# A two-layer decoder trunk on one core: convolution taps behind the second group of attention scores instead of ahead of the first, and the last memory queries transposed within the attention

## The chip, the cores and the metric

The kernel runs on one NeuronCore of a Trainium2 chip. The core has a matrix engine (TensorE, PE in the profile, with PEld for its weight loads), a vector engine (VectorE, DVE), a scalar engine (ScalarE, ACT), GpSimd (POOL) and a queue engine (SyncE, SP) that only issues transfers. Each engine works through its own list of instructions in order and waits at an instruction until what it needs is there. The metric is the device time of one execution in microseconds; lower is better.

## The reference

Two layers. Each has a half-step feed-forward block, a mixer, a second half-step feed-forward block and a closing norm. The mixer projects 512 tokens once and splits the columns among three groups of heads:

```python
def reference(x, mem, ...):
    for l in range(DEPTH):                                     # 2 layers, 512 tokens x 1024
        h = x + 0.5 * swiglu(rms_norm(x, ffn1_norm[l]), ...)   # 1024 -> 2816 -> 1024
        p = rms_norm(h, mix_norm[l]) @ w_in[l]
        u_conv, q, k, v, q_mem = jnp.split(p, splits, axis=-1)
        y_conv = conv_module(u_conv, ...)          # GLU, 31 causal taps on 384 channels, LayerNorm, silu
        y_swa = sliding_window_attention(q, k, v, sinks)       # 6 heads of 64, window 128
        y_mem = memory_attention(qm, mk, mv)                   # 4 heads of 64 on 256 memory tokens
        h = h + jnp.concatenate([y_conv, y_swa, y_mem], -1) @ w_out[l]
        h = h + 0.5 * swiglu(rms_norm(h, ffn2_norm[l]), ...)
        x = rms_norm(h, final_norm[l])
```

## The kernel before

All products with weights are made as three float32r matmuls of split operands (`mm3`, lines 177 to 179: high by high, high by low, low by high). The feed-forward blocks take most of the time and are PE's; the change is in the mixer (`mixer`), once in each layer.

The mixer's work is written in the order of a table, `ORDER`. `c` is half of a convolution channel group's projection (`conv_half`), `q` the projection of the attention's queries and keys of a block of 128 tokens (`queries`), `Q` their transposition into columns (`query_columns`), `v` the projection of the values and of the memory's queries of a block (`values`), `V` the transposition of that block's memory queries (`value_columns`, line 573 on PE), `g0` and `g1` the scores of the first two groups of heads (`begin`), `a` the attention, `t0` to `t2` the taps of a channel group, `s` what follows the convolution (`swish`).

The attention runs over ten groups (`GROUPS`). "r" groups are memory attention on two pairs of heads, "w" groups window attention on one to three pairs. For each group PE makes scores (line 755, behind masks of line 749 for "w"), DVE takes their maxima (lines 759 or 774) and turns them into a bias (lines 760, or 775 and 776), which also needs the norm factor `rm` that POOL raises to a power (line 546). Then, pair by pair, ACT takes the exponential (line 786), PE transposes it (line 792), ACT evicts the transposes into the ring `ptb` (line 794), and PE multiplies them with the values in narrow products of 65 columns (line 803). DVE divides (lines 812 to 817), PE transposes the result (line 826), and ACT and DVE split it into an operand (lines 146 and 147). Each group's scores are made while the group before is worked on.

The 31 taps on each of three channel groups are 93 instructions of DVE over 128 x 512 (line 912 the first of a channel group, line 919 the others). A tap's place is set by hand. The taps are numbered 0 to 92 through the three channel groups. Those below `EARLY` may go as soon as their input is there; the others are put behind the bias of a score group (`biased`), as many behind each group as `LATER` says, and the rest behind the last one. A scheduler fixes each engine's list when the program is built, within these ties.

The memory queries of block t are written by ACT (line 721, out of the same PSUM tile as the values, line 719) into `scratch[0]`, 256 columns for each block, and read by PE for their transposition (line 573). The ring `ptb` is made of the two halves of the same `scratch[0]`. So the transposes of blocks 2 and 3 have to be done before `ptb` gets its second half. Block 2's were at `V2`, ahead of the attention, block 3's within the attention, behind the transposes of the first pair of the first group.

When the last tap is done, POOL adds up the three channel groups (lines 925 and 926), PE sums over the channels (line 930), and DVE, ACT and PE make the norm, while PE goes on with the output projection of the attention's part (`out_rows`).

Of the kernel before, what the change touches and what calls it, by code (L numbers as in the profile page):

```python
# [43 lines left out]
MAGIC = 12582912.0  # L44


ORDER = "c00 c01 q0 c10 q1 c11 Q0 q2 q3 Q1 c20 c21 Q2 v0 Q3 v1 V0 V1 g0 g1 v2 v3 V2 a t0 t1 t2 s"

EARLY = 50
LATER = (5, 5, 4, 4, 3, 3, 3, 3, 3, 3)  # L50


def cut(v, bits):
# [11 lines left out]
def trunk(ctx: ExitStack, tc: tile.TileContext, xT, memT, pos, w1a, w3a, w2a, w1b, w3b, w2b,  # L65
# [118 lines left out]
    def blk(k, n=P):  # L184
        return slice(k * n, (k + 1) * n)
# [383 lines left out]
    def to_columns(dst, src, n, tag="pt"):  # L569

        pt = bank([P, n, P], tag)
        for c in range(n):
            tail[0] = T.transpose(pt[:, c, :], src[:, blk(c)], ident)
        if dst is not None:
            A.activation(dst, pt[:, 0 : dst.shape[1], :], AF.Copy)
        return pt
# [38 lines left out]
    def mixer(l, x, st, last):  # L615
# [9 lines left out]
        qmT = there[:, 0:1024].rearrange("p (i s) -> p i s", i=2)  # L625
        cv = there[:, 1024:2560].rearrange("p (c s) -> p c s", c=CC)
        G.memset(vn[:, :, :, HD : HD + 1], 1.0)
        scratch = [wst.tile([P, UNIT], F32, tag="aux", name=f"aux{i}", bufs=3) for i in range(3)]
        uu = tmp.tile([P, 2, S], F32, tag="u", name="uu", bufs=1)
        query = [tmp.tile([P, 2, S], F32, tag="g", name="query", bufs=2) for _ in range(2)]  # L630
# [78 lines left out]
            keyed.append(A.activation(kT[:, blk(t)], pt[:, CC, :], AF.Copy, scale=HD**-0.5))  # L709


        def values(t):
            if not t:
                ww["v"] = [weights(wvm[l, i], 768, G if i == 2 else V, spare()) for i in range(4)]
            ps = mm() if t < 2 else bank([P, S], "po")
            with queued():
                for k in range(KD):
                    mm3(ps[:, 0:CCH], at(x, ALL, k, blk(t)), at(ww["v"][k // 2], ALL, blk(k % 2, CCH)), k == 0, k == KD - 1)
            A.activation(vn[:, t, :, 0:HD], heads(ps[:, 256:CCH]), AF.Copy, scale=rc[:, t : t + 1])
            q = scratch[0][:, blk(t, 256)]  # L720
            A.activation(q, ps[:, 0:256], AF.Copy, scale=rc[:, t : t + 1])
            head_scale(ps[:, 0:256], rc[:, t : t + 1], NM, rm[:, t, :])

        def value_columns(t):
            with queued():
                to_columns(qmT[:, :, blk(t)], scratch[0][:, blk(t, 256)], 2)

        yy, y = [], []

# [113 lines left out]
        def attention():  # L843
# [23 lines left out]
            for n, (kind, *pairs) in enumerate(GROUPS):  # L867
                ready = list(done)
                done.clear()
                final = n + 1 == len(GROUPS)  # L870
                if final:

                    for r in ready:
                        attended(*r)
                    ready = []
                elif n + 1 not in begun:
                    begin(n + 1)
                if n in (3, 5):
                    with tc.issue_after(raised[GROUPS[n - 1][0], *GROUPS[n - 1][-1]].ins):
                        out_weights(len(out_w))  # L880
                for z, (b, c) in enumerate(pairs):
                    x = turned(kind, b, c, [ps[:, z, :] for ps in begun[n][0]], begun[n][1])
                    close()
                    late = (kind, b, c, *x)
                    if not n and not z:
                        value_columns(3)
                for r in ready:
                    attended(*r)
            out_rows(0, MEMORY)
# [21 lines left out]
        def taps(c):  # L911
            V.tensor_scalar(out=cv[:, c, :], in0=ypad[:, c, 0:S], scalar1=conv_w[:, c, 0:1], scalar2=conv_b[:, c : c + 1],
                            op0=ALU.mult, op1=ALU.add)
            for j in range(1, TAPS):

                n = c * TAPS + j - EARLY
                group = sum(n >= sum(LATER[:g]) for g in range(1, len(LATER)))
# [34 lines left out]

        for step in ORDER.split():
            f = {"c": conv_half, "q": queries, "Q": query_columns, "v": values, "V": value_columns, "g": begin, "a": attention,
# [148 lines left out]
```

## Time and profile before

| | us |
|---|---|
| median of three runs (1811.9, 1816.54, 1817.14) | 1816.54 |
| the profiled execution | 1813.94 |
| its span in the trace | 1812.2 |
| of it, attention of layer 1 (444 to 512) | 68 |
| of it, attention of layer 2 (1339 to 1404) | 65 |

Two microseconds of the profiled execution lie outside its span. Times in a row are from the span's start. A timeline row has the start, the time taken, the engine, the line of the kernel, the operation, what it writes and reads, and how many instructions stand in the row; in brackets how long the engine had idled before it, and which engine, tile and line ended that. "64*128 64x256" of a matmul are its stationary and moving operand. A float32 product, as of lines 755 and 803, stands in the trace as two passes, so eight rows there are four products. PE's records overlap: in a series the distance from start to start is what one costs. The granted clock is the share of full speed that PE was given.

### The profile page before, as it was taken

How to read it: one execution, taken by the hardware profiler on the slowest of the kernel's cores; microseconds unless marked ns; L12 is line 12 of the kernel's file. 1: busy time of each engine (PE TensorE's matmuls, PEld its weight loads, DVE VectorE, ACT ScalarE, POOL GpSimd, SP SyncE). 2: the span in 40 equal slices, each digit the busy share in tenths (PEclk: the TensorE clock that was granted, in tenths of full speed). 3: DMA queues.
4: the chain of work that ended last, by engine and by line, in shares of the span. 5: the costliest groups of instructions: out<-in, count | busy, mean ns of one | idle time of the engine just before them, and what ended most of it. 6: DMA issues, size and time to landing. Idle time of an engine off the chain costs nothing.

```text
span 1812.2 us, 28077 instructions
## 1 busy us (share of the span) xinstructions
PE 1769.9 (98%) x10996; PEld 1587.2 (88%) x10996; DVE 1273.0 (70%) x1886; ACT 897.1 (50%) x1363; POOL 205.8 (11%) x225
## 2 busy tenths in 40 slices
PE   8999999999999999999999999999989999999997
PEld 6989999878778989898888898988777789898986
DVE  7969666569757857575678676666698567675755
ACT  5546444463665535353655453535446645453532
POOL 3001000024121000000010010000341210000000
PEclk9999999999899999999999999999999999999998
DMA  9456655282159456565566465643631866474622
GB/s 275 106 167 169 180 136 143 59 224 69 30 131 211 112 140 173 137 163 140 154 138 154 147 172 144 171 120 95 175 69 30 207 149 161 131 181 119 173 75 81
DMA packets 96180, 254.37 MB, mean 140 GB/s; under 512 B 9904, under 2 KB 14256, under 8 KB 96048
## 3 DMA queue, kind: packets, MB, share of 16 engines
q1 hardware_dynamic: 77040, 190.45, 34.3%
q0 software_dynamic: 19008, 62.14, 19.4%
q8 instruction: 86, 1.41, 0.3%
q14 instruction: 46, 0.38, 0.1%
HBM read 250.45 MB, written 2.10 MB: 139 GB/s over the span
## 4 chain that ended last, share of the span: by engine, by line
PE 78%; DVE 9%; issue 6%; DMA 4%; ACT 3%; SPq 0%; POOLq 0%; DVEq 0%; POOL 0%; ACTq 0%
PE mm L177 11%; PE mm L178 11%; PE mm L179 11%; PE po L177 8%; PE po L179 8%; PE po L178 8%; PE pt L177 6%; PE pt L178 6%; PE pt L179 6%; DVE there L919 3%; DVE wlo L147 1%; DMA raw<-in_wconv 1%; PE po L803 1%; DMA glo<-in_wqk 1%; ACT uu L786 1%
## 5 line engine op out<-in xcount | busy, mean ns | idle before, releaser
L146 ACT ACTIVATE whi<-raw 128x1024 fp32r<-128x1024 f32 (+3 forms) x344 | 324.6, 946 | 454.6 <-PE mm L178 232.6
L147 DVE TENSOR_TENSOR wlo<-raw,whi 128x1024 fp32r<-128x1024 f32 (+3 forms) x344 | 372.7, 1085 | 132.3 <-ACT whi L146 131.5
L178 PE MATMUL mm<-glo,whi 128*128 128x512 f32 x752 | 293.7, 391 | 1.0 <-DVE glo L147 1.0
L177 PE MATMUL mm<-ghi,whi 128*128 128x512 f32 x752 | 293.4, 392 | 0.7 <-ACT ghi L146 0.7
L179 PE MATMUL mm<-ghi,wlo 128*128 128x512 f32 x734 | 285.8, 389 | 0.0
L179 PE MATMUL po<-mh,wlo 128*128 128x256 f32 x864 | 244.6, 283 | 1.4 <-DVE wlo L147 1.4
L177 PE MATMUL po<-mh,whi 128*128 128x256 f32 x864 | 244.8, 283 | 0.0
L178 PE MATMUL po<-ml,whi 128*128 128x256 f32 x864 | 244.5, 283 | 0.0
L179 PE MATMUL pt<-xhi,wlo 128*128 128x256 f32 x864 | 244.0, 283 | 0.0
L177 PE MATMUL pt<-xhi,whi 128*128 128x256 f32 x864 | 243.3, 283 | 0.7 <-DVE g L370 0.4
L178 PE MATMUL pt<-xlo,whi 128*128 128x256 f32 x864 | 243.9, 283 | 0.0
L467 DVE SCALAR_TENSOR_TENSOR h<-mm,h 128x512 f32<-128x512 f32 x128 | 87.8, 689 | 134.6 <-PE mm L179 134.6
L178 PEld LDWEIGHTS mm<-glo,whi 128*128 128x128 f32 x752 | 141.3, 188 | 31.1 <-DVE glo L147 2.8
L177 PEld LDWEIGHTS mm<-ghi,whi 128*128 128x128 f32 x752 | 141.3, 188 | 31.1 <-ACT ghi L146 1.6
L179 PEld LDWEIGHTS po<-mh,wlo 128*128 128x128 f32 x864 | 165.8, 192 | 1.6 <-DVE wlo L147 1.6
L177 PEld LDWEIGHTS pt<-xhi,whi 128*128 128x128 f32 x864 | 165.1, 192 | 2.2 <-ACT xhi L146 0.7
L177 PEld LDWEIGHTS po<-mh,whi 128*128 128x128 f32 x864 | 165.8, 192 | 0.9 <-ACT part L389 0.2
L178 PEld LDWEIGHTS pt<-xlo,whi 128*128 128x128 f32 x864 | 165.7, 192 | 0.8
L178 PEld LDWEIGHTS po<-ml,whi 128*128 128x128 f32 x864 | 165.8, 192 | 0.6
L179 PEld LDWEIGHTS pt<-xhi,wlo 128*128 128x128 f32 x864 | 165.6, 192 | 0.0
L179 PEld LDWEIGHTS mm<-ghi,wlo 128*128 128x128 f32 x734 | 137.8, 188 | 28.7
L919 DVE SCALAR_TENSOR_TENSOR there<-ypad,par,there 128x512 f32<-128x512 f32 x180 | 135.2, 760 | 1.8
(314 smaller groups left out, 3341.8 us busy)
## 6 DMA issues: line engine op xcount, KB each, us to landing
raw<-in_w2a SPq DMA_DIRECT2D x48, 384.0 KB, 3.6
raw<-in_w2b SPq DMA_DIRECT2D x48, 384.0 KB, 3.6
raw<-in_w1b SPq DMA_DIRECT2D x26, 512.0 KB, 3.7
raw<-in_w3b SPq DMA_DIRECT2D x26, 512.0 KB, 3.9
raw<-in_w1a SPq DMA_DIRECT2D x25, 512.0 KB, 3.7
raw<-in_w3a SPq DMA_DIRECT2D x25, 512.0 KB, 4.2
wsum<-in_w1a SPq DMA_DIRECT2D x18, 512.0 KB, 4.5
wsum<-in_w3a SPq DMA_DIRECT2D x18, 512.0 KB, 4.5
```

Of the source, the lines that this page charges most:

```text
L146: A.activation(hi, x, AF.Copy)
L147: on.tensor_tensor(out=lo, in0=x, in1=hi.bitcast(F32), op=ALU.subtract)
L177: T.matmul(ps, a[0], b[0], start=first, stop=False, **more)
L178: T.matmul(ps, a[0], b[1], start=False, stop=False, **more)
L179: tail[0] = T.matmul(ps, a[1], b[0], start=False, stop=last, **more)
L467: added = V.scalar_tensor_tensor(out=h[:, d, :], in0=ps, scalar=0.5, in1=h[:, d, :], op0=ALU.mult, op1=ALU.add)
L786: raised[kind, b, c] = A.activation(pr[:, i, 0:W], scores[i], AF.Exp, bias=nm[:, b, i, c : c + 1], scale=rr[:, b, n : n + 1])
L803: tail[0] = T.matmul(po[:, 2 * c + i, :], ptb[:, i, j, :], v, start=(j == 0), stop=(j == nk - 1))
L919: V.scalar_tensor_tensor(out=cv[:, c, :], in0=ypad[:, c, j : j + S], scalar=conv_w[:, c, j : j + 1], in1=cv[:, c, :], op0=ALU.mult, op1=AL ...
```

## The change

Three things change together.

1. `EARLY` goes from 50 to 43, so seven taps fewer are free to go ahead of the first groups' maxima. `LATER` goes from (5, 5, 4, 4, 3, ...) to (1, 12, 5, 4, 3, ...): one tap behind the first group's bias in place of five, twelve behind the second's in place of five, five behind the third's in place of four; behind the last group's come 13 in place of 10.
2. `V2` leaves `ORDER`. The transposes of memory queries 2 and 3 are both made within the attention, behind the first pair of the second and of the third group.
3. The memory queries of blocks 2 and 3 are kept in a part of `query[0]`, whose earlier contents have been used by then, so that they no longer share `scratch[0]` with the ring `ptb`.

```diff
-ORDER = "... v2 v3 V2 a t0 t1 t2 s"
-EARLY = 50
-LATER = (5, 5, 4, 4, 3, 3, 3, 3, 3, 3)
+ORDER = "... v2 v3 a t0 t1 t2 s"
+EARLY = 43
+LATER = (1, 12, 5, 4, 3, 3, 3, 3, 3, 3)
...
+        def memory_query(t):
+            return (scratch[0] if t < 2 else query[0][:, 0])[:, blk(t % 2, 256)]
+
         def values(t):
...
-            q = scratch[0][:, blk(t, 256)]
+            q = memory_query(t)
...
         def value_columns(t):
             with queued():
-                to_columns(qmT[:, :, blk(t)], scratch[0][:, blk(t, 256)], 2)
+                to_columns(qmT[:, :, blk(t)], memory_query(t), 2)
...
-                    if not n and not z:
-                        value_columns(3)
+                    if n in (1, 2) and not z:
+                        value_columns(n + 1)
```

Line numbers behind line 712 are three higher in the changed kernel: 755 becomes 758, 786 789, 792 795, 803 806, 919 922.

The first place is DVE's list around the first two groups' maxima, in layer 1. `hs` and `hv` are the sums of squares of the memory queries (4240 and 4281 those of blocks 0 and 1), `there<-ypad` is a tap, `nmr` the maxima and biases of the memory groups. Before:

```order
L912 TENSOR_SCALAR there<-ypad,par 128x512
L542 TENSOR_REDUCE hs_4240<-hsq 128x4
L919 SCALAR_TENSOR_TENSOR there<-ypad,par,there 128x512
L543 TENSOR_SCALAR hv_4241<-hs_4240 128x4
L919 SCALAR_TENSOR_TENSOR there<-ypad,par,there 128x512 x3
L542 TENSOR_REDUCE hs_4281<-hsq 128x4
L919 SCALAR_TENSOR_TENSOR there<-ypad,par,there 128x512
L543 TENSOR_SCALAR hv_4282<-hs_4281 128x4
L919 SCALAR_TENSOR_TENSOR there<-ypad,par,there 128x512
L759 TENSOR_REDUCE nmr<-mm 128x2
L919 SCALAR_TENSOR_TENSOR there<-ypad,par,there 128x512
L759 TENSOR_REDUCE nmr<-mm 128x2 x2
```

With the change, from the same first row to the second group's bias and the taps behind it:

```order
L915 TENSOR_SCALAR there<-ypad,par 128x512
L542 TENSOR_REDUCE hs_4240<-hsq 128x4
L543 TENSOR_SCALAR hv_4241<-hs_4240 128x4
L542 TENSOR_REDUCE hs_4281<-hsq 128x4
L543 TENSOR_SCALAR hv_4282<-hs_4281 128x4
L762 TENSOR_REDUCE nmr<-mm 128x2 x2
L763 SCALAR_TENSOR_TENSOR nmr<-nmr,rm 128x4
L922 SCALAR_TENSOR_TENSOR there<-ypad,par,there 128x512
L762 TENSOR_REDUCE nmr<-mm 128x2
L762 TENSOR_REDUCE nmr<-cf 128x2
L763 SCALAR_TENSOR_TENSOR nmr<-nmr,rm 128x4
L922 SCALAR_TENSOR_TENSOR there<-ypad,par,there 128x512 x5
```

The six taps that stood between the first channel sum and the first maximum, and the one between the first group's two maxima, are gone from there. Twelve taps now lie between the second group's bias and the third group's maxima, mixed with the sums of blocks 2 and 3.

The second place is PE's list behind the last product of `values(3)`, and ACT's list that feeds it. `uu` and `pr` are exponentials, `mvn` the memory's values, `here` holds the queries' columns, `aux_3742` is `scratch[0]`. PE before:

```order
L179 MATMUL po<-ghi,xlo 128x384
L573 MATMUL pt<-cst,aux_3742 128x128 x2
L792 MATMUL pt<-cst,uu 128x128 x4
L573 MATMUL pt<-cst,aux_3742 128x128 x2
L792 MATMUL pt<-cst,uu 128x128 x4
L803 MATMUL po<-mvn,aux_3742 128x65 x4
L749 MATMUL mm<-maskr 128x384 x2
L755 MATMUL mm<-here 128x128 x6
```

PE with the change:

```order
L179 MATMUL po<-ghi,xlo 128x384
L795 MATMUL pt<-cst,uu 128x128 x8
L806 MATMUL po<-mvn,aux_3742 128x65 x4
L752 MATMUL mm<-maskr 128x384 x2
L758 MATMUL mm<-here 128x128 x6
L795 MATMUL pt<-cst,pr 128x128 x4
L806 MATMUL po<-mvn,aux_3742 128x65 x4
L573 MATMUL pt<-cst,query 128x128 x2
```

ACT with the change, from its table load on:

```order
L789 ACT_TABLE_LOAD
L789 ACTIVATE uu<-mm,nmr,rm 128x256 x4
L789 ACTIVATE pr<-mm,nmr,rm 128x256
L789 ACTIVATE pr<-cf,nmr,rm 128x256
L722 ACTIVATE here<-po,rc 128x2x64
L724 ACTIVATE query<-po,rc 128x256
L540 ACTIVATE hsq<-po,rc 128x256
L722 ACTIVATE here<-po,rc 128x2x64
L724 ACTIVATE query<-po,rc 128x256
L540 ACTIVATE hsq<-po,rc 128x256
L789 ACTIVATE uu<-mm,nmr,rm 128x256
L797 ACTIVATE aux_3742<-pt 128x512
```

The transposes of the memory queries have gone from between those of the exponentials, and the eight transposes of the first group follow `values(3)` at once. On ACT the rows up to the second `hsq` stand as before; the eviction of block 2's memory queries (line 575), which stood between the last `hsq` and the next exponential, has moved behind the third group's first exponentials.

The third place is DVE's list at the end of the attention, where `rd_4834` and the row L817 (L820 with the change) make the last block's result and L147 splits its transposes. Before:

```order
L813 RECIPROCAL rd_4834<-rd_4834 128x6
L919 SCALAR_TENSOR_TENSOR there<-ypad,par,there 128x512
L817 TENSOR_TENSOR aux_3743<-po,rd_4834 128x384
L147 TENSOR_TENSOR glo<-pt,ghi 128x128
L147 TENSOR_TENSOR glo<-pt,ghi 128x2x128
```

With the change:

```order
L816 RECIPROCAL rd_4834<-rd_4834 128x6
L922 SCALAR_TENSOR_TENSOR there<-ypad,par,there 128x512
L820 TENSOR_TENSOR aux_3743<-po,rd_4834 128x384
L922 SCALAR_TENSOR_TENSOR there<-ypad,par,there 128x512 x2
L147 TENSOR_TENSOR glo<-pt,ghi 128x128
L922 SCALAR_TENSOR_TENSOR there<-ypad,par,there 128x512
L147 TENSOR_TENSOR glo<-pt,ghi 128x2x128
```

The last three taps stand behind the last division instead of ahead of it.

More of the change, by code (lines that the diff above doesn't have):

```diff
@@ L44 @@
 MAGIC = 12582912.0
-ORDER = "c00 c01 q0 c10 q1 c11 Q0 q2 q3 Q1 c20 c21 Q2 v0 Q3 v1 V0 V1 g0 g1 v2 v3 V2 a t0 t1 t2 s"
-EARLY = 50
-LATER = (5, 5, 4, 4, 3, 3, 3, 3, 3, 3)
+ORDER = "c00 c01 q0 c10 q1 c11 Q0 q2 q3 Q1 c20 c21 Q2 v0 Q3 v1 V0 V1 g0 g1 v2 v3 a t0 t1 t2 s"
+EARLY = 43
+LATER = (1, 12, 5, 4, 3, 3, 3, 3, 3, 3)
 def cut(v, bits):
```

## The prediction

> **What bounds the kernel now.** I read the page first.
>
> ```profile
> span 1812.2 us, 28077 instructions
> PE 1769.9 (98%) x10996; PEld 1587.2 (88%) x10996; DVE 1273.0 (70%) x1886; ACT 897.1 (50%) x1363; POOL 205.8 (11%) x225
> ```
>
> A PE that is busy 98% of 1812.2 us leaves little to win, unless it is busy slowly somewhere. So the second view is the window table, for stretches of 3.41 us (the trace's falls and returns of the clock lie a multiple of that apart) and for the time at half clock. Columns: length, busy time of PE, weight loads, DVE, ACT, POOL, then the granted clock.
>
> ```profile
> 454.51:457.92 3.41, 1.15 (x9) 0.83 (x8) 3.13 (x7) 3.41 (x10) 0.00 (x0) 1.00 0.00 0
> 457.92:474.99 17.07, 16.30 (x76) 13.40 (x75) 9.10 (x20) 8.37 (x21) 5.33 (x5) 0.50 0.18 38
> 502.29:505.71 3.42, 2.33 (x20) 1.88 (x19) 3.42 (x8) 2.26 (x7) 0.56 (x1) 1.00 0.00 0
> 1352.21:1355.62 3.41, 1.31 (x8) 0.84 (x9) 3.18 (x7) 3.41 (x11) 1.05 (x1) 1.00 0.00 0
> 1355.62:1362.45 6.83, 6.80 (x35) 6.17 (x36) 3.30 (x9) 1.86 (x5) 1.70 (x3) 0.50 0.01 2
> 21.01:24.43 3.42, 2.50 (x15) 1.92 (x15) 3.41 (x4) 1.06 (x1) 2.45 (x3) 1.00 0.61 126
> ```
>
> In the attention of layer 1 PE runs at half clock for 17.07 us, in that of layer 2 for 6.83 us, each time behind a stretch in which it was busy 1.15 or 1.31 us of 3.41. The timeline of PE shows what emptied it; the second row below is the last product of values(3).
>
> ```profile
> 444.72 1.34 PE L755 MATMUL mm<-mT,there 64*128 64x256 f32 x9 [0.20 <-ACT there L575]
> ...
> 454.92 0.34 PE L179 MATMUL po<-ghi,xlo 128*128 128x384 f32 x1
> 457.52 0.44 PE L573 MATMUL pt<-cst,aux 128*128 128x128 f32 x2 [2.26 <-ACT aux L721]
> ```
>
> PE waits 2.26 us for ACT to evict values(2), and ACT is late since the exponentials ahead of it waited for DVE's first maxima:
>
> ```profile
> 452.70 1.28 ACT L786 ACT_TABLE_LOAD   x1 [7.76 <-DVE nmr L760]
> 454.00 1.93 ACT L786 ACTIVATE uu<-mm,nmr,rm 128x256 f32<-128x256 f32 x4
> ...
> 457.68 0.42 ACT L719 ACTIVATE here<-po,rc 128x128 f32<-128x128 f32 x1
> ...
> 458.64 0.45 ACT L575 ACTIVATE there<-pt 128x256 f32<-128x256 f32 x1
> 458.91 0.65 ACT L786 ACTIVATE uu<-mm,nmr,rm 128x256 f32<-128x256 f32 x1
> 459.36 0.68 ACT L794 ACTIVATE aux<-pt 128x512 f32<-128x512 f32 x1
> ```
>
> DVE has the other half of the story (L919 is a tap, L774 a maximum over PE's scores):
>
> ```profile
> 444.44 0.53 DVE L912 TENSOR_SCALAR there<-ypad,par 128x512 f32<-128x512 f32 x1
> 444.90 0.40 DVE L542 TENSOR_REDUCE hs<-hsq 128x4 f32<-128x256 f32 x1
> ...
> 450.01 0.68 DVE L759 TENSOR_REDUCE nmr<-mm 128x2 f32<-128x512 f32 x1
> ...
> 451.28 1.28 DVE L759 TENSOR_REDUCE nmr<-mm 128x2 f32<-128x512 f32 x2
> 452.47 0.15 DVE L760 SCALAR_TENSOR_TENSOR nmr<-nmr,rm 128x4 f32<-128x4 f32 x1
> ...
> 454.58 3.11 DVE L919 SCALAR_TENSOR_TENSOR there<-ypad,par,there 128x512 f32<-128x512 f32 x4
> ...
> 465.23 1.02 DVE L774 TENSOR_REDUCE nmw<-mm 128x3 f32<-128x384 f32 x2 [3.39 <-PE mm L755]
> ...
> 473.30 0.69 DVE L774 TENSOR_REDUCE nmw<-mm 128x2 f32<-128x512 f32 x1 [3.60 <-PE cf L755]
> ...
> 1360.70 1.02 DVE L774 TENSOR_REDUCE nmw<-mm 128x3 f32<-128x384 f32 x2 [3.39 <-PE mm L755]
> ...
> 1365.86 0.69 DVE L774 TENSOR_REDUCE nmw<-mm 128x2 f32<-128x512 f32 x1 [1.04 <-PE cf L755]
> ```
>
> First scores are begun at 444.72, yet their maximum starts at 450.01: seven taps stand ahead of it. Later DVE has used up its taps and waits 3.39 and 3.60 us for a slow PE. Behind that it is the bound; these two windows reach from the third group's maxima to the last eviction that PE waits for (the DVE row below):
>
> ```profile
> 465.23:505.19 39.96, 37.99 (x265) 31.60 (x265) 34.31 (x82) 28.71 (x67) 6.89 (x9) 0.88 0.16 34
> 1360.70:1397.16 36.46, 34.26 (x265) 28.64 (x265) 34.28 (x82) 28.61 (x67) 6.90 (x9) 0.98 0.17 37
> ```
>
> ```profile
> 504.77 0.42 DVE L147 TENSOR_TENSOR glo<-pt,ghi 128x256 fp32r<-128x256 f32 x1
> ...
> 510.69 0.55 DVE L817 TENSOR_TENSOR aux<-po,rd 128x384 f32<-128x384 f32 x1
> ```
>
> ```profile
> 505.25 0.66 PE L792 MATMUL pt<-cst,uu 128*128 128x128 f32 x4 [0.49 <-DVE glo L147]
> ...
> 514.98 1.02 PE L930 MATMUL pt<-aux,onesq 128*128 128x512 f32 x2
> ```
>
> DVE is busy 34.3 us in both layers; the 3.5 us between them are PE's clock. From 505.25 on PE's products follow each other almost without a hole, so what is saved before 505 stays saved.
>
> **The change, step by step** (layer 1's clock; layer 2 runs 895.47 us later, as 1360.70 against 465.23 shows).
>
> First maxima. With seven taps fewer ahead of them DVE waits only for the scores, done by 444.72 + 1.34 = 446.1. Two reductions take 1.28 (row 451.28), the bias 0.15: ready at 447.5. It also needs POOL's power, begun once the sum of 444.90 is scaled, about 445.6:
>
> ```profile
> 446.13 1.52 POOL L546 TENSOR_TENSOR rm<-hv,nhalf 128x4 f32<-128x4 f32 x1 [6.90 <-DVE hv L543]
> ...
> 510.92 1.29 POOL L926 TENSOR_TENSOR aux<-aux,there 128x512 f32<-128x512 f32 x1 [8.07 <-DVE there L919]
> ```
>
> It ends at 447.1, under the reductions. ACT's table load moves from 452.70 to 447.6, five us earlier, and its six exponentials are over by 451.8.
>
> PE behind values(3), which still ends at 454.92 + 0.34 = 455.26, now has eight transposes of finished exponentials in place of the memory queries'. I price them, and what follows at full clock, by the rows on the right side of the trace:
>
> ```profile
> 476.70 0.71 PE L749 MATMUL mm<-maskr 128*128 128x512 f32 x2
> 477.34 1.14 PE L755 MATMUL mm<-here 64*128 64x256 f32 x8
> 478.41 0.66 PE L792 MATMUL pt<-cst,uu 128*128 128x128 f32 x4
> ...
> 483.09 1.00 PE L803 MATMUL po<-here,aux 128*128 128x65 f32 x8
> ```
>
> Four transposes take 0.49 start to start, eight 0.98: to 456.24. Then PE needs ACT's first eviction of them. ACT's order puts the three evictions of values(3) and one exponential ahead of it: 457.68 to 460.04 in the rows above, less 0.27 for the L575 that has moved back, is 2.09 us, now counted from PE's 455.30. So the eviction ends at 457.4 and PE idles **1.2 us in place of 2.26**. Eight narrow products (0.85), two masks of 384 columns (0.4, half of what they take at half clock) and twelve passes of scores (0.8) bring the third group's scores to 459.5. DVE is there too: second group's bias at 449.6, twelve taps at 0.75 (four take 3.11), two small sums (0.9) make 459.5. **The third group's maxima start at 459.5 instead of 465.23.**
>
> From there DVE needs its 34.3 us, one tap more (five behind the third group for four, 0.7) and the waits that remain without slow PE: in layer 2, 36.46 - 34.28 = 2.18, less the 1.04 and 0.2 that PE's clock caused, 0.9. Sum 35.9. It ends at 495.4 instead of 505.19, **9.8 us gained**; in layer 2 at 1354.97 + 35.9 = 1390.9 instead of 1397.16, **6.3 us gained**.
>
> Given back: three taps more stand behind the last group's maxima, and all three fall behind L817. The last tap ends 2.85 us behind L817's start (0.47 for it, two taps, a short eviction, one tap), at 513.55 on the old clock; POOL's sum starts 0.23 later and takes 1.29, to 515.1, where PE arrives at 514.98; the eviction between the taps is 0.2 late. About 0.3 us a layer, at most 2.3 if PE had no other work there. Sum: -9.8 - 6.3 + 0.6 = **-15.5 us** against the profiled execution's own 1813.94: 1798.4. The moved transposes cost nothing more: as many as before, four of them now in PE's full stretch. The median of the runs, 1816.54, lies 2.6 above the profiled one, within their spread of 5.2; part of that spread must be the clock, which the change calms. I add 1: **1799**.
>
> The unknown in this sum is the clock. Worst is a 3.41 us stretch that holds the whole hole: busy 3.41 - 1.2 = 2.2 us. The clock held behind a stretch with 2.33 busy (502.29). It fell behind 1.15 and 1.31, and at 21.01 behind 2.50, but 1.05 of these were products of a single column:
>
> ```profile
> 23.29 1.05 PE L203 MATMUL cf<-onesq,st 128*128 128x1 f32 x8 [0.92 <-DVE st L249]
> ```
>
> which leaves 1.45. So 2.2 is nearest to the row that held. I take full clock, and keep the other end: at half clock from 457.9 on, the third group's scores come at 461.2, and from there PE needs what it needed before (465.23 to 473.30, or 1360.70 to 1365.86 in layer 2) and 0.4 for two moved transposes. That gains 3.6 us a layer instead of 9.8 and 6.3. The Trainium skill (TensorE: Matmul & The Clock Gate, "Why this matters for your kernels") asks for no gap of PE above some 3 us, since a whole idle window sends the clock back to half. By that rule a hole of 2.26 us is not the cause, and filling it need not bring the clock back: the sum would be -6.6, the second case below. The trace disagrees: the one hole over 1 us at that place is of 2.26, and 0.50 follows.
>
> **Rivals.**
>
> *The clock still falls in one layer, or in both.* What counts towards it may be less than busy time. For: eight transposes stand at that place, and 1352.21, mostly transposes, fell. Against: 502.29 held, and PE does nothing there but transposes and narrow products. Time: 2.7 (layer 2) to 6.2 (layer 1) more than the forecast, 1802 to 1805; in both layers 1808. The Trainium skill (same page, Part 4: PE-mode transpose) has a rule for it, that transposes do not count as busy; by it the worst stretch holds 1.2 us and the clock falls in both layers. Row 502.29 speaks against it.
>
> *Nothing to measure.* Half clock in both layers, and five stretches of it in layer 2 as in layer 1: layer 2 then loses (473.30 - 465.23) - (1365.86 - 1360.70) = 2.9 of its 3.6, and the sum is about -3.7: 1810 on the profiled execution, 1813 on the median. The change would not do what it is said to do, since DVE would wait for PE as before with its taps elsewhere.
>
> *Slower: the clock falls and does not come back within the attention.* In 465.23:505.19 PE is busy 37.99 us at a mean of 0.88, 33.4 us of full clock; at half that is 66.9, or 27 more. The start at 461.2 gives back 4.0 and the other layer 6.3, so 1799 + 9.8 - 4.0 + 27 = 1832. It decides from four more stretches at half clock than the seven of now (1.7 us each, half of 3.41, against 7.2 that are saved in any case), and is measurable from seven more. Against: both layers recovered, on the same masks and scores.
>
> **How the numbers follow.** Full clock in both layers 0.55 (1799); half clock in one 0.22 (1802 to 1805), in both 0.10 (1808); nothing to measure 0.07; slower 0.06. A measurement of this kernel can tell about 0.3%, 5.4 us, from no change. So faster 0.87, same 0.07, slower 0.06. The range takes the first three cases and the spread of the runs on the low side: 1794 to 1809.
>
> **What the new profile would show.** Table load at 447.6, PE's hole behind values(3) of 1.2 us, third group's maxima at 459.5, clock 1.00 throughout, DVE without a wait over 0.5 us until 495, POOL's last sum 1.3 us behind the last tap with PE waiting for it 0.3 us or less. A first eviction later than 457.6, or clock 0.50 behind it, would prove the sum wrong; a gain of 16 us with half clock in the rows would prove the reason wrong.

## The result, and the profile after

| | before | changed |
|---|---|---|
| median of five runs, us | 1811.9 (1810.73 to 1817.14) | 1801.53 (1800.64 to 1805.25) |
| the profiled execution, us | 1813.94 | 1801.14 |
| its span, us | 1812.2 | 1799.4 |

The ratio is 0.9942, with a 95% interval of 0.9921 to 0.9962: 0.6% faster. (Two more runs of before brought its median down from the 1816.54 shown above.) Between the two profiled executions it is 12.8 us.

The page of the changed kernel, span and engines:

```profile
span 1799.4 us, 28071 instructions
...
PE 1760.2 (98%) x10996; PEld 1579.0 (88%) x10996; DVE 1275.6 (71%) x1886; ACT 897.5 (50%) x1363; POOL 205.7 (11%) x225
```

PE is busy 9.7 us less with as many instructions: they ran at a higher clock. DVE is busy 2.6 us more, also with as many instructions; that is followed up below.

The timeline of the changed kernel at the same places, one fence for each engine. First PE, with the last product of values(3), the hole behind it, and the sum over the channels (L933, which was L930 at 514.98):

```profile
455.30 0.34 PE L179 MATMUL po<-ghi,xlo 128*128 128x384 f32 x1
455.47 1.03 PE L795 MATMUL pt<-cst,uu 128*128 128x128 f32 x8
457.77 1.10 PE L806 MATMUL po<-mvn,aux 128*128 128x65 f32 x8 [1.26 <-ACT aux L797]
...
507.04 1.02 PE L933 MATMUL pt<-aux,onesq 128*128 128x512 f32 x2
```

ACT, with its table load and its first eviction of transposes:

```profile
447.94 1.28 ACT L789 ACT_TABLE_LOAD   x1 [2.63 <-DVE nmr L763]
...
455.67 0.37 ACT L722 ACTIVATE here<-po,rc 128x128 f32<-128x128 f32 x1 [2.59 <-PE po L179]
...
457.10 0.61 ACT L797 ACTIVATE aux<-pt 128x512 f32<-128x512 f32 x1
```

DVE, from the first tap of the third channel group to the last tap:

```profile
444.81 0.53 DVE L915 TENSOR_SCALAR there<-ypad,par 128x512 f32<-128x512 f32 x1
...
446.31 1.28 DVE L762 TENSOR_REDUCE nmr<-mm 128x2 f32<-128x512 f32 x2
...
460.18 1.02 DVE L777 TENSOR_REDUCE nmw<-mm 128x3 f32<-128x384 f32 x2
...
468.67 1.65 DVE L922 SCALAR_TENSOR_TENSOR there<-ypad,par,there 128x512 f32<-128x512 f32 x1
...
504.65 0.74 DVE L922 SCALAR_TENSOR_TENSOR there<-ypad,par,there 128x512 f32<-128x512 f32 x1
```

The first tap of the third channel group, 444.44 before, is at 444.81 here, so 0.37 us has to be taken off a time of this trace to set it beside one of before. ACT's table load has come forward from 452.70 to 447.94, PE's hole behind values(3) has gone from 2.26 to 1.26 us, the third group's maxima from 465.23 to 460.18, and no wait of 3.39 or 3.60 us is left on DVE.

The window table of the changed kernel (length, busy time of PE, weight loads, DVE, ACT, POOL, then the granted clock): the 3.41 us that hold PE's hole; the stretch from the third group's maxima to the end of the eviction that PE waits for, in both layers; and two rows from between the layers:

```profile
455.10:458.51 3.41, 2.15 (x19) 1.87 (x17) 3.30 (x7) 2.84 (x7) 1.49 (x1) 1.00 0.00 0
460.18:497.02 36.84, 34.10 (x269) 28.31 (x269) 35.72 (x83) 29.20 (x69) 7.98 (x10) 1.00 0.19 37
905.66:909.07 3.41, 3.15 (x23) 2.86 (x22) 0.57 (x4) 3.25 (x4) 1.53 (x2) 1.00 0.22 23
909.07:912.49 3.42, 3.42 (x10) 2.64 (x9) 0.33 (x2) 0.65 (x1) 2.35 (x3) 0.50 0.88 226
1348.93:1385.79 36.86, 34.09 (x269) 28.32 (x269) 35.74 (x83) 29.19 (x69) 7.67 (x10) 1.00 0.19 37
```

The clock stays full in both attentions, and the stretches, 39.96 and 36.46 us before, are now alike. Between the layers one new stretch at half clock has come (909.07), which costs half of 3.41, 1.7 us. It comes in some executions and not in others, of this kernel too (last section).

From the first tap of the third channel group to PE's sum over the channels it was 70.54 us in layer 1 (444.44 to 514.98) and 67.04 in layer 2; now it is 62.23 (444.81 to 507.04) and 62.23. That is 8.31 and 4.81, **13.12 us won in the two attentions**. The rest of the program is 0.3 us longer: 0.37 ahead of the first attention, 1.59 between the two (the new stretch), and 1.65 shorter at the end, where half clock lasts 9.7 us (1789.71 to 1799.4) instead of 12.8.

### The profile page after: what moved, and what is told of

The parts are those of the page before. It is cut to its first block, busy times and chain, and to the rows that moved or that the text cites. A ratio compares the mean times of both kernels' runs of the same rounds, so it can differ in the third digit from the quotient of the medians.

```text
span 1799.4 us, 28071 instructions
## 1 busy us (share of the span) xinstructions
PE 1760.2 (98%) x10996; PEld 1579.0 (88%) x10996; DVE 1275.6 (71%) x1886; ACT 897.5 (50%) x1363; POOL 205.7 (11%) x225
## 4 chain that ended last, share of the span: by engine, by line
PE 79%; DVE 8%; issue 6%; ACT 3%; DMA 3%; SPq 0%; POOLq 0%; DVEq 0%; POOL 0%; ACTq 0%
PE mm L177 11%; PE mm L178 11%; PE mm L179 11%; PE po L177 9%; PE po L179 9%; PE po L178 9%; PE pt L177 6%; PE pt L178 6%; PE pt L179 6%; DVE there L922 3%; DVE wlo L147 1%; PE cf L177 1%; PE cf L179 1%; DMA glo<-in_wqk 1%; PE cf L178 1%
## 5 line engine op out<-in xcount | busy, mean ns | idle before, releaser
L147 DVE TENSOR_TENSOR wlo<-raw,whi 128x1024 fp32r<-128x1024 f32 (+3 forms) x344 | 372.7, 1085 | 136.0 <-ACT whi L146 134.9
```

The costliest lines, as they stand in the source:

```text
L147: on.tensor_tensor(out=lo, in0=x, in1=hi.bitcast(F32), op=ALU.subtract)
```

## The experiments

Where nothing else is said these are medians of 5 to 12 runs, each with a ratio against the kernel before, run beside it. "Attention" is the time from the first tap of the third channel group to PE's sum over the channels, and "maxima" that from the same tap to the third group's maxima, in layers 1 and 2 of the profiled execution.

| | median, us | ratio (95%) | maxima | attention | half clock in it, us |
|---|---|---|---|---|---|
| before | | | 20.79, 20.79 | 70.54, 67.04 | 17.07, 6.83 |
| changed | 1801.53 | 0.9942 (0.9921 to 0.9962) | 15.37, 15.37 | 62.23, 62.23 | 0, 0 |
| transposes alone | 1813.27 | 0.9991 (0.9975 to 1.0006) | 19.70, 18.71 | 67.26, 69.68 | 6.83, 13.65 |
| taps alone | 1802.04 | 0.9937 (0.9919 to 0.9955) | 16.09, 16.08 | 62.58, 62.60 | 0, 0 |
| before, hole filled | 1805.27 | 0.9946 (0.9926 to 0.9966) | 19.42, 18.53 | 65.49, 63.95 | 3.41, 0 |
| no first sum (one run) | 1801.48 | | 15.37, 15.36 | 61.90, 61.87 | 0, 0 |
| changed again | 1800.76 | 0.9929 (0.9912 to 0.9945) | 15.97, 15.35 | 63.75, 62.22 | 3.41, 0 |
| changed, hole filled | 1799.36 | 0.9933 (0.9913 to 0.9953) | 15.35, 15.32 | 62.20, 62.18 | 0, 0 |

### Which half of the change does it: transposes alone, taps alone

Transposes alone is the changed kernel with the old table:

```diff
-EARLY = 43
-LATER = (1, 12, 5, 4, 3, 3, 3, 3, 3, 3)
+EARLY = 50
+LATER = (5, 5, 4, 4, 3, 3, 3, 3, 3, 3)
```

> The changed kernel with the old table of taps (50 free, then 5, 5, 4, 4, 3, ...); the transposes of memory queries 2 and 3 stay where the change put them. Theory A (the early maxima do the work): the first maxima start near 450.0 as before, ACT's table load is at about 452.7, and since ACT's queue is as late as before, PE has its eight transposes behind values(3) and then waits until about 459.7 for the first eviction, a hole of some 3.4 us in place of 2.26; the clock falls in both layers and the time is 0 to 5 us below the kernel before. Rival B (the transposes alone shorten the hole enough): the hole is 1.3 us or less, the clock stays at 1.00 in the attention, and the time is 9 to 12 us below.

The timeline of that kernel, ACT's table load and PE behind values(3), and its windows ahead of and at half clock:

```profile
452.55 1.28 ACT L789 ACT_TABLE_LOAD   x1 [7.75 <-DVE nmr L763]
...
459.66 1.75 PE L806 MATMUL po<-mvn,aux 128*128 128x65 f32 x7 [3.39 <-ACT aux L797]
```

```profile
454.85:458.27 3.42, 1.42 (x10) 0.83 (x8) 3.15 (x6) 3.42 (x11) 0.00 (x0) 1.00 0.00 0
458.27:465.09 6.82, 5.43 (x28) 4.77 (x29) 4.37 (x10) 2.28 (x6) 2.50 (x2) 0.50 0.00 0
1352.56:1366.21 13.65, 13.50 (x62) 11.36 (x63) 6.58 (x16) 5.95 (x15) 4.76 (x5) 0.50 0.12 28
```

The hole is 3.39 us, as expected, the clock falls in both layers, and nothing is won. With ACT as late as before, the eight transposes do not fill the hole: they run ahead of it, and the wait for the eviction comes in one piece.

Taps alone is the kernel before with the new table, `V2` and the buffers where they were:

```diff
-EARLY = 50
-LATER = (5, 5, 4, 4, 3, 3, 3, 3, 3, 3)
+EARLY = 43
+LATER = (1, 12, 5, 4, 3, 3, 3, 3, 3, 3)
```

> The kernel before with the new table of taps (43 free, then 1, 12, 5, 4, 3, ...); the transposes of memory queries 2 and 3 stay in their old places and in scratch[0]. Theory A: ACT's table load is at 447.9, memory query 2 has been evicted before PE has done values(3), so PE goes on at 455.6 with its transposes; two short holes are left (about 0.6 us for memory query 3, 1.0 us for the first eviction). The clock stays full, the third group's maxima start at about 460.8 (0.6 later than with the whole change), and the time is 10 to 12 us below the kernel before, within 2 us of the whole change. Rival B: the clock falls in at least one layer and half or less of the gain is left, 0 to 6 us.

Its timeline, ACT's table load and PE behind values(3):

```profile
448.63 1.28 ACT L786 ACT_TABLE_LOAD   x1 [2.64 <-DVE nmr L760]
...
457.78 0.44 PE L573 MATMUL pt<-cst,aux 128*128 128x128 f32 x2 [0.81 <-ACT there L575]
458.82 0.63 PE L792 MATMUL pt<-cst,uu 128*128 128x128 f32 x4 [0.60 <-ACT aux L794]
```

Two holes of 0.81 and 0.60 us take the place of one of 2.26, the clock stays full, and the time is that of the whole change. The maxima are 0.7 us later than with it and the attention 0.35 us longer in each layer: that is what moving the transposes adds, and only a trace shows it. **The taps do the work**; the transposes' new place is worth little with them and nothing without them.

### Is it the clock: the hole filled in the kernel before

```diff
         def value_columns(t):
+            if t == 2:
+                with queued():
+                    fill = bank([P, S], "pt")
+                    for i in range(2):
+                        tail[0] = T.matmul(fill, onesq, ypad[:, 0, 0:S], start=i == 0, stop=i == 1)
```

> The kernel before, taps and transposes as they were, with two extra float32 products of 512 columns (some 1.8 us of PE, into a PSUM tile that nobody reads) in PE's list between values(3) and the transposes of memory query 2, where PE idled 2.26 us. Theory C (the lost time of before is the clock's, and the clock fell for that hole): the clock stays at 1.00 in both attentions; PE then waits about 1 us for ACT's first eviction (it ends near 460.0), the third group's maxima start at about 462.4 in place of 465.23 and the DVE stretch behind them takes 36 to 37 us; 7.0 us less in layer 1 and 3.4 in layer 2, so 9 to 11 us below the kernel before without any tap moved. Rival D (the gain comes from where the taps stand, and a hole under 3 us is not why the clock fell): clock 0.50 as before and a time within 2 us of the kernel before.

The timeline of PE there (the extra products are L729), and its windows:

```profile
455.28 1.88 PE L729 MATMUL pt<-ypad,onesq 128*128 128x512 f32 x4
457.73 0.44 PE L573 MATMUL pt<-cst,aux 128*128 128x128 f32 x2 [0.57 <-ACT aux L721]
```

```profile
458.51:461.93 3.42, 2.06 (x16) 1.77 (x16) 3.31 (x7) 3.07 (x8) 1.50 (x1) 1.00 0.00 0
461.93:465.35 3.42, 3.42 (x21) 2.78 (x21) 1.35 (x5) 0.19 (x1) 1.01 (x1) 0.50 0.00 0
```

No tap moved, and two products whose result nobody reads save 0.5% (0.3 to 0.7): 5.05 us of attention in layer 1 and 3.09 in layer 2, 8.1 of the 13.1 that the change wins there. So most of the time that before lost is the clock's, and the clock falls for holes well under 3.4 us. Theory C had no fall at all, and 9 to 11 us; the medians, 1813.17 and 1805.27, are 7.9 apart. In layer 1 one stretch of 3.41 us fell later, behind 2.06 us of busy PE, since the waits for ACT's evictions that follow (0.76 and 0.60 us) were not filled. That is part of why layer 1's maxima came at 464.05 and not at 462.4: they are 19.42 us behind the first tap, and 18.53 in layer 2, where nothing fell. The other 0.6 us (462.4 would be 17.96 behind the first tap) is not the clock's; theory C had priced the way to the maxima too short.

### What POOL's first sum costs beside a tap

In the changed kernel one tap took 1.65 us (468.67 above), where others take 0.75. POOL at that time, and its last sum for comparison, in the changed kernel's timeline:

```profile
468.05 1.72 POOL L928 TENSOR_TENSOR aux<-there 128x512 f32<-128x512 f32 x1
...
505.53 1.28 POOL L929 TENSOR_TENSOR aux<-aux,there 128x512 f32<-128x512 f32 x1 [10.84 <-DVE there L922]
```

In before the first sum stood at 469.44, within one of DVE's long waits, and took 1.27. The test leaves it out:

```diff
-            G.tensor_tensor(out=s1, in0=cv[:, 0, :], in1=cv[:, 1, :], op=ALU.add)
-            G.tensor_tensor(out=s1, in0=s1, in1=cv[:, 2, :], op=ALU.add)
+            G.tensor_tensor(out=s1, in0=cv[:, 0, :], in1=cv[:, 2, :], op=ALU.add)
```

> The changed kernel without POOL's first sum over channel groups (POOL adds groups 0 and 2 only, group 1 is left out of the norm's mean). In the changed kernel the tap that runs beside that sum takes 1.65 us (468.67 to 470.32, and 1357.42 to 1359.07 in layer 2) where others take 0.75, and the sum 1.72 where it took 1.27. Theory E (DVE and POOL slow each other down): without the sum all taps there take 0.75, the stretch from the third group's maxima to the last eviction that PE waits for takes 35.9 us in place of 36.84 in both layers, and the time is about 1.8 us below the changed kernel. Rival F (that tap is slow for another reason): it takes 1.65 again and the stretch 36.8.

DVE's timeline without the sum, and the window from the third group's maxima on:

```profile
466.82 2.19 DVE L922 SCALAR_TENSOR_TENSOR there<-ypad,par,there 128x512 f32<-128x512 f32 x3
469.51 0.69 DVE L777 TENSOR_REDUCE nmw<-mm 128x2 f32<-128x512 f32 x1 [0.49 <-PE mm L758]
```

```profile
459.78:496.29 36.51, 34.11 (x269) 28.32 (x269) 34.90 (x83) 29.19 (x69) 6.28 (x9) 1.00 0.18 37
```

Three taps take 2.19 us, where the same three took 3.09 in the changed kernel (467.23), so theory E is right that the two engines slow each other down. That is also where most of DVE's 2.6 us more went: without the sum it is busy 1272.8 us in the whole execution, as before (1273.0). Theory E's sum is not: DVE is busy 0.82 us less (34.90 against 35.72), but the stretch is shorter by 0.33 only (36.51 against 36.84), since DVE now waits 0.49 for PE's scores. The same small gain stands in both attentions (62.23 to 61.90 and 61.87), and the one run shows no difference from the changed kernel.

### How safe the full clock is: the changed kernel again, and with its hole filled

> The changed kernel once more, beside the next three on one chip. Expected: 10 to 13 us below the kernel before, the clock at 1.00 in both attentions, the tap beside POOL's first sum at 1.65 us again. In the first trace the 3.41 us that held PE's hole (455.10 to 458.51) had 2.15 us of busy PE and the clock held, while a stretch with 2.06 fell in the kernel with the filled hole: if the edge lies there, this execution, with the stretches elsewhere, may show one stretch of 0.50 in an attention and 1 to 3 us more.

The windows of this execution around PE's hole in layer 1:

```profile
454.28:457.69 3.41, 2.15 (x18) 1.66 (x17) 3.34 (x7) 2.71 (x7) 0.82 (x1) 1.00 0.00 0
457.69:461.11 3.42, 3.42 (x23) 3.20 (x23) 2.61 (x6) 0.87 (x3) 1.99 (x2) 0.50 0.00 0
```

Instruction for instruction the program is the same, the hole is again 1.26 us, and PE is again busy 2.15 us of 3.41, but here the clock fell. The two stretches cut the same work at different points, 0.8 us apart against the first tap (443.15 here): the one that held has all eight transposes in it, the one that fell about half of them, and instead more of the narrow products and masks behind the hole. It costs 1.5 us (63.75 against 62.23), and the control further down fell in the same way.

Three more executions have the same instructions up to this place: the kernel without the first sum and, further down, two of the version with three taps more. That makes six executions and, with both layers, twelve holes of this kind. The clock fell behind two of them, where the stretch that holds most of the hole begins 11.13 and 11.14 us behind the first tap. It held behind the ten where that stretch begins 9.0 to 10.81 us behind it, and five of these had no more than 2.15 to 2.17 us of busy PE. So the hole that is left is safe at most places of a stretch and not at all of them. Filling it as well:

```diff
                     po[kind, b] = bank([P, NH if kind == "w" else NM, HD + 1], "po")
+                    if len(po) == 1:
+                        with queued():
+                            for _ in range(2):
+                                tail[0] = T.matmul(po[kind, b].rearrange("p n e -> p (n e)")[:, 0:256], onesq, ypad[:, 0, 0:256],
+                                                   start=True, stop=True, skip_group_check=True)
```

> The changed kernel with two extra float32 products of 256 columns (some 0.9 us of PE) between the eight transposes behind values(3) and the first narrow products, where PE idles 1.26 us. The same kernel without them held the clock there in one execution and lost one stretch of 3.41 us in layer 1 in two others (379.19 and 457.69; 380.67 and 459.18 in the control), with 2.15 us of busy PE ahead of it each time. Theory C: with about 3.0 us busy in that stretch no attention falls in this execution, and the third group's maxima start 15.4 us behind the first tap of the third channel group in both layers; the time is that of the changed kernel less up to 1.5 us. Rival D: it falls in some executions all the same (15.9 or more in a layer), or the extra products, not hidden, push the maxima back by 0.9 us.

Its timeline and its window at that place (L863 are the extra products):

```profile
455.66 1.03 PE L863 MATMUL po<-ypad,onesq 128*128 128x256 f32 x4
457.08 1.11 PE L806 MATMUL po<-mvn,aux 128*128 128x65 f32 x8 [0.39 <-ACT aux L797]
```

```profile
455.55:458.96 3.41, 3.02 (x24) 2.32 (x24) 3.34 (x7) 2.42 (x6) 0.76 (x2) 1.00 0.00 0
```

The products are hidden (maxima at 15.35 and 15.32, as without them) and both attentions ran at full clock, as theory C expects. One execution does not prove that they always do, and the medians, 1799.36 and 1800.76, are not apart by their intervals.

### What bounds it now: a control and three versions

Theory G says that DVE's own work up to the last tap is the bound now, so that time saved on PE has to be used for something. The control moves only PE's sum over the channels (`pm`) behind the second row of the output projection. `EARLY` and `LATER` are as in the change unless shown.

```diff
             out_rows(0, OWN)
+            out_rows(1, OWN)
             pm = bank([P, S], "pt")
...
-            out_rows(1, OWN)
             out_rows(2, OWN)
```

> The changed kernel with PE's sum over the channels put 9 products (2.05 us) later in PE's list, behind the second row of the output projection; nothing else. Theory G (up to that sum the attention is bound by DVE's own work, some 58 of 61 us): PE had no wait there, so nothing is won: within 1 us of the changed kernel, and the sum stands 2.05 us later with 2 us of slack behind the last tap. It is the control for the next two. Rival: the norm's chain behind the sum is late everywhere then, and the time is 2 to 4 us above.

1802.04 in one run, with layer 1's clock fallen once, for 1.5 us: nothing won and nothing lost. With three taps more behind the last group:

```diff
-LATER = (1, 12, 5, 4, 3, 3, 3, 3, 3, 3)
+LATER = (1, 12, 5, 4, 3, 3, 2, 2, 2, 3)
```

> As the control, and three taps more moved from behind groups 7, 8 and 9 to behind the last group (16 there in place of 13). Theory G: DVE is the bound within the attention, so PE's attention gets 1 to 1.5 us shorter in each layer, the last tap ends when it ended, PE uses the time for the products ahead of the sum: 2 to 3 us below the changed kernel. Rival H (PE's and ACT's chain of scores, exponentials and transposes is as tight as DVE, as the kernel without POOL's first sum hints, which got 0.33 us for 0.9): 0.3 us or less in a layer, within 1 us of the changed kernel.

> The kernel with three taps more behind the last group and the sum over the channels 9 products later, once more, beside the other two on one chip: 12 to 14 us below the kernel before (12.8 between medians the first time), PE's wait for the sum about 0.6 us, and 1 to 3 us below the changed kernel.

1798.91, ratio 0.9920 (0.9903 to 0.9936), and the second time 1799.39, 0.9926 (0.9905 to 0.9946). Its timeline at the sum over the channels:

```profile
505.15 1.73 POOL L929 TENSOR_TENSOR aux<-aux,there 128x512 f32<-128x512 f32 x1 [13.41 <-DVE there L922]
...
506.93 1.12 PE L934 MATMUL pt<-aux,onesq 128*128 128x512 f32 x2 [0.64 <-POOL aux L929]
```

From the third group's maxima to the start of the eviction that PE waits for it takes 35.68 us in both layers instead of 36.43, so 0.75 of the three taps' 2.2 us is won there: between theory G and rival H. It does not last to the sum. The last tap ends 62.4 us behind the first tap of the third channel group, where it ended 60.6 behind it (theory G had it end as before), and PE waits 0.64 us for the sum; 0.45 of that is POOL's last sum, which takes 1.73 us beside DVE's splitting of weights instead of 1.28. From that first tap to PE's sum it is 64.3 us in both layers of both executions, and so are the changed kernel's 62.23 with the 2.05 by which the sum was moved back: up to the sum nothing is won.

It is the fastest version tried. Its median is 1.85 us below the changed kernel's beside it, 1.4 to 2.1 below the second time (the changed kernel was not run beside it then), and the intervals do not separate the two. But for the start and the end of the program, its two profiled executions have one stretch at half clock each (at 907), the two of the changed kernel two each (25.02 and 909.07; 379.19 and 457.69). At 1.7 us each that is as much as the difference, and the three at 25.02, 379.19 and 457.69 lie ahead of the place where the two kernels part. What else the difference would come from is not shown.

The next one has ACT evict the first group's transposes ahead of values(3) (whose three evictions are called behind `turned`, tied to the first eviction of `ptb`), with `pm` as in the control:

```diff
-LATER = (1, 12, 5, 4, 3, 3, 3, 3, 3, 3)
+LATER = (1, 10, 5, 4, 3, 3, 3, 2, 2, 3)
...
                     x = turned(kind, b, c, [ps[:, z, :] for ps in begun[n][0]], begun[n][1])
+                    if held and not n and not z:
+                        with tc.issue_after(evicts[-1].ins):
+                            held.pop()()
```

> As the control; ACT evicts the first group's transposes ahead of values(3) instead of behind it, and ten taps in place of twelve stand behind the second group's bias (and one less behind groups 8 and 9), four more behind the last group. Theory G: PE's hole behind values(3) shrinks from 1.26 us to 0.3 or less, the third group's maxima start 14.3 us behind the first tap of the third channel group in place of 15.37, the stretch from there is 1.2 us shorter, and the time is 3 to 5 us below the changed kernel. Rival H: the earlier start is given back in the stretch behind, at most 1 us a layer is left, 0 to 2 us below.

PE's timeline behind values(3) and at the sum over the channels:

```profile
455.08 1.11 PE L815 MATMUL po<-mvn,aux 128*128 128x65 f32 x8 [0.55 <-ACT aux L806]
...
507.44 1.12 PE L946 MATMUL pt<-aux,onesq 128*128 128x512 f32 x2 [1.55 <-POOL aux L941]
```

The hole shrinks to 0.55 us and the maxima come 0.7 us earlier (14.65; theory G had 0.3 and 14.3), but PE then waits 1.55 us for the sum: 1801.26, ratio 0.9936 (0.9917 to 0.9956), no better than the change. In layer 2 the clock falls at 1405.88, not behind that wait (1395.64:1399.06, with 2.12 us of busy PE, held) but behind products of a single column, of which the last section tells more. The last attempt puts `pm` one row further back, to have that wait filled:

```diff
             out_rows(1, OWN)
+            out_rows(2, OWN)
             pm = bank([P, S], "pt")
...
-            out_rows(2, OWN)
```

> As the kernel with the eviction ahead of values(3)'s, and PE's sum over the channels put another 9 products (2.05 us) back, behind the third row of the output projection. There PE waited 1.55 us a layer for that sum, and the clock fell behind it once. Theory G (what was won in the attention was given back at that wait): the wait is gone, 2 to 4 us less than that kernel's 1801.3, that is 1797 to 1799. Rival: the norm's chain behind the sum is late by as much, PE waits before its last loop of the output projection, and the time stays at 1800 to 1802.

The timeline of PE at the sums of squares, in both layers:

```profile
515.60 1.05 PE L203 MATMUL cf<-onesq,st 128*128 128x1 f32 x8 [2.30 <-DVE st L249]
...
1407.29 0.94 PE L203 MATMUL cf<-onesq,st 128*128 128x1 f32 x7 [2.52 <-DVE st L249]
```

The wait did not go, it moved: 2.30 and 2.52 us at the next thing that DVE delivers. The clock falls in both layers too (518.62 and 1409.50), behind a stretch with the rest of that wait and 1.95 us of the single-column products above. 1805.19, ratio 0.9955 (0.9937 to 0.9973), the slowest of these. The rival had it right that nothing is won, but its 1800 to 1802 was still too low. What holds of theory G is that DVE's chain, taps, sum, norm, sets the end, and PE pays at one of its waits for it. What fell is that a later place of PE's sum makes that free.

## Why the prediction came out right

The forecast was 1799 with a range of 1794 to 1809; the median is 1801.53. By its own steps (times of the changed kernel less 0.37):

- **First maxima, table load.** Foreseen 447.6, measured 447.57. Right, and the taps-alone run shows that it carries the gain.
- **Hole behind values(3).** Foreseen 1.2 us, with the first eviction over at 457.4; measured 1.26 and 457.34. The transposes that I had fill it are not what matters: the taps alone do as well with two short holes.
- **Third group's maxima.** Foreseen 459.5, measured 459.81. From the first narrow product to the maxima it took 2.41 us (457.77 to 460.18), not 2.05.
- **The DVE stretch.** Foreseen 35.9 in both layers, measured 36.84 and 36.86. This is the term that was mis-sized. Its first part, DVE's 34.3 us and one tap, took POOL's first sum as costing DVE nothing, which it did only while DVE was waiting; now it costs a tap 0.9 us. Its second part, waits of 0.9 us, was short too: without the sum DVE is busy 34.90 but the stretch is 36.51, that is 1.6 us of waits. Of the 0.94 us that were missing, 0.33 go with the sum, 0.6 with these waits.
- **Given back at the end.** Foreseen 0.3 us a layer. Measured: the stretch ends 8.54 us earlier (505.19 to 497.02, and 0.37), PE's sum 8.31, so 0.23.
- **Sum.** Foreseen 9.5 us won in layer 1 and 6.0 in layer 2, 15.5 together; measured 8.31 and 4.81, 13.12 together, less 0.3 lost elsewhere. So the profiled execution is 1801.14 and not 1798.4. The step from there to a median was of about the right size (1 foreseen, 0.4 measured), but it was taken from a median of before of 1816.54 that two more runs brought down to 1811.9: against medians the forecast was 17.5 us, and 10.4 came.
- **The clock.** Full in both attentions of the first trace, as forecast, but the reason, that 2.2 us of busy PE is nearest to the row that held, was too good: with 2.15 to 2.17 it held five times and fell twice, and where the stretch begins against the program made the difference. That the first trace was among those that held was in part luck. The rival "falls in one layer" happened in two of the six executions with this hole. It was mis-sized: it costs 1.5 us and not 2.7 to 6.2, because it lasts one stretch and not two to five. So it did not decide between fast and slow.
- **The Trainium skill's rule on gaps** (TensorE: Matmul & The Clock Gate, "Why this matters for your kernels"), by which a hole of 2.26 us is not the cause, is not borne out: filling that hole alone brought 8.1 us of attention back. **Its rule on transposes** (same page, Part 4: PE-mode transpose), read by the prediction as that they do not count as busy, is not borne out in that form: without its 1.03 us of transposes 455.10:458.51 has some 1.1 us of busy PE, no more than the stretches that fell in before, and it kept its clock. In 455.63:459.04 of taps alone (last section) all but 0.5 of 2.00 us are transposes, and the clock held too. Whether they count for less than other products stays open.
- **The rivals.** "Nothing to measure" needed a DVE that waits for a slow PE as before; transposes alone (0.9991) is what that looks like. "Slower" needed a clock that does not come back, and no execution showed that.

## What to carry to other kernels

When an engine is idle in the middle of its critical stretch, look at what it would have to be handed for that to go, and by whom: here PE idled for ACT, ACT for DVE, and DVE was busy with taps that could run anywhere else, so a table of numbers on DVE was the remedy for PE's clock. Before a stretch is priced as "the same work without the waits", look at what other engines did during those waits, since it will now run beside the work. A wait that was filled by moving work behind it came back here at the next thing that the same engine delivered; it helps only if that engine has less to do, or the time is needed elsewhere.

## What the runs showed of the hardware

**Busy time alone does not tell when the clock falls.** Busy PE in the 3.41 us ahead of a fall in an attention was 1.15 and 1.31 us (before), 1.42 and 0.17 (transposes alone), 2.06 (before, hole filled) and 2.15 (changed again, and the control). Stretches with 2.15 (changed) and 2.33 (before) held, and so did some with less. The first is of taps alone, the second of before with its hole filled (layer 2), the third of the last version above:

```profile
455.63:459.04 3.41, 2.00 (x14) 1.52 (x14) 3.30 (x7) 2.68 (x8) 1.49 (x1) 1.00 0.00 0
```

```profile
1349.40:1352.81 3.41, 2.05 (x17) 1.61 (x16) 3.20 (x6) 3.27 (x10) 1.50 (x1) 1.00 0.00 0
```

```profile
511.79:515.21 3.42, 1.51 (x7) 0.93 (x5) 0.76 (x2) 3.01 (x5) 1.13 (x2) 1.00 0.57 127
```

The last of them, with 1.51 us, holds nothing but products of 512 columns with weights; the clock was still full in the stretch behind it. Between the layers, on the other hand, it fell behind 3.15 us of busy PE (905.66:909.07 above). The timeline of PE in that stretch of the changed kernel:

```profile
906.30 0.95 PE L203 MATMUL cf<-onesq,st 128*128 128x1 f32 x8
907.51 1.05 PE L203 MATMUL cf<-onesq,RL 128*128 128x1 f32 x8 [0.26 <-DVE ms L209]
```

Two of the 3.15 us are products of a single column, and without them 1.15 us are left, as in the stretch that fell in before; such products seem to count for little. The other executions bear that out. In eight of the thirteen profiled, both rows lie in one stretch (to within 0.11 us), and the clock fell behind it each time; in the other five an edge between two stretches cuts them, and it held. Over all thirteen executions, of the stretches with 0.9 us or more of single-column products (line 203), all those with 1.45 us or less of other products were followed by half clock, and all those with 1.51 or more held, but for two near 377 (1.66 and 1.75). What exactly is counted was not measured and stays open: 2.15 us of transposes, narrow products and masks fell, 1.51 of projections held.

Where the stretches lie against the program differs from execution to execution, and with it where the clock falls: at 909.07 in one execution of the changed kernel, at 379.19 and 457.69 in another. These falls are worth about 1.7 us each, as much as the smaller edits here.

**POOL and DVE block each other over operands in SBUF.** A tap (0.75 us alone) took 1.65 us and the sum (1.27 alone) 1.72 where they met; a last sum beside DVE's splitting of weights took 1.73 instead of 1.28. The sum began at 468.05, 0.6 us ahead of the end of the tap before (the slow one follows at 468.67), and lost 0.45; the slow tap began 1.1 us ahead of the sum's end (468.05 + 1.72), and lost 0.9: as if each waited for most of the other's instruction. The Trainium skill (SBUF — State Buffer, "SBUF: two separate sides") says the same, that the two engines' shared ports are an exclusive lock held for the whole instruction by a DVE operation with two SBUF inputs or by one of GpSimd. This trace agrees in the main: 0.45 and 0.9 us were lost where such a lock would cost 0.6 and 1.1.
